# All stores of the last two turned blocks on SyncE's queue, and four operand rings of the w_up stage laid out in another order

## The chip, the cores and the metric

The kernel runs on one core of a Trainium2 chip. The metric is the device time of one launch in microseconds (us). Before the change it is 2649.21 us, the median of 3 runs that lie between 2648.27 and 2650.63 us.

## What is computed

One layer of an encoder on 2048 tokens of 1024 features, in float32. Cut to what this case needs:

```python
h  = rms_norm(x, norm_mix)
z  = h @ w_in                                  # queries, keys, values and gates of two attentions
yA = windowed_gqa(...)                         # window of 128 tokens
yB = neighborhood_attn(...)                    # on a 32 x 64 grid of tokens
merged = sigmoid(gA) * (yA @ w_proj_a) + sigmoid(gB) * (yB @ w_proj_b)
x  = x + merged @ w_out
h2 = rms_norm(x, norm_mlp)
x  = x + square(relu(h2 @ w_up)) @ w_down      # w_up is 1024 x 4096, w_down 4096 x 1024
out = rms_norm(x, norm_final)
```

## The kernel before

**Stages.** TensorE does the input projection and the attentions (to 1060 us of the span), the gated projections and w_out (matmuls named `pgl` until 1394.8 us), w_up (from 1395.0 to 2030 us) and w_down (2032 to 2642 us). The case is about the seam between w_out and w_up.

**Operands.** Every float32 factor is split in a high part (a rounding, ScalarE, `CAST` in the helper at L283) and a low part (what the rounding lost, VectorE, L284), and each 128x128 by 128x512 product is three matmuls: high by high (L287), high by low (L288), low by high (L289).

**w_up by seven products.** Tokens and features are taken as 2 by 2 blocks, and seven products of sums of blocks replace eight. For each half `m` of the tokens (1024 each) and each eighth `q` of w_up's 4096 columns, `up_quad` does the products in the order 1, 5, 6, 2, 7, 4, 3. A product is 24 matmuls: two PSUM banks, four slices, three matmuls. Its weights come from `up_left_steps` (tiles `uwhla`, `uwhlb`). Its other factor is a *page*, a pair of tiles `ubh` (high and low, each cast in two pieces), made by `up_right` once for each half `m`. In the listings below pages have these numbers: page 6 is 13477 and 13478, page 2 is 13485 and 13486, page 7 is 13563 and 13564, page 4 is 13571 and 13572, page 3 is 13577 and 13578. The weights of the first eighth's products 7, 4 and 3 are 13500, 13503 and 13507; `uwhlb_13825` is the weight of product 1 of the second eighth, made from the load `uraw_13583`. Banks 13643 and 13658 hold products 6, 7 and 4, and are read out between them (`uc`, L280).

**The turned blocks.** At the end of w_out the rows of x (`xr`, 128 tokens by 1024 features) are complete. Each is stored (`x2d`, L173, on ScalarE's queue), its squares are summed (L223, ScalarE, with a small VectorE and a GpSimd step), and it is scaled in place (L235, ScalarE). `turned_out` then transposes four rows on VectorE (L247) into a buffer of 4 KB a partition and stores that buffer as four pieces of 128 KB into `h2d` (L256), in runs of 512 bytes. For the third block of tokens (`turned_last(0, ...)`) the buffers are `m2` and `m3`, which w_out no longer needs; for the fourth (`turned_last(1, ...)`) they are `hu`. Each of these blocks has 16 such stores. `turned_last` gives two of each four to SyncE and two to ScalarE. What is stored is read again only by the work for the second half of the tokens.

**Who lies over what.** The rings of w_up are taken from the space that w_out's buffers leave. When `m0` to `m3` and `pgl` are closed, pages 6 and 2, `rb` and `c` take that space, so page 6 can be written once the stores of the third block have landed. When `hu` and `xr` are closed, `up_homes` makes four rings there, one below the other: pages 7, 4 and 3 and the small buffers `chunk`. A tile of a new ring waits for whatever still uses the old bytes.

**Order.** Each engine works through its instructions in the order in which a scheduler put them when the program was built, and an instruction that waits holds up all behind it on its engine. A DMA that SyncE or ScalarE issues takes the next of eight semaphores (`DMAHW0` to `DMAHW7`) in turn and waits until the DMA that had it before has landed.

Of the kernel before, what the change touches and what calls it, by code (L numbers as in the profile page):

```python
# [92 lines left out]
def encoder_layer(ctx, tc, x, norm_mix, w_in, b_gate, sink, rpb, w_pa, w_pb, w_out,  # L93
                  norm_mlp, w_up, w_down, norm_final, dist_a, mask_b, out):
    nc = tc.nc
    V, A, G, PE, SY = nc.vector, nc.scalar, nc.gpsimd, nc.tensor, nc.sync
# [27 lines left out]
    def T(pl, shape, dt, tag, bufs):  # L124
        n_t[0] += 1
        pl = pl[tag] if isinstance(pl, dict) else pl
        return pl.tile(shape, dt, tag=tag, bufs=bufs, name=f"{tag}_{n_t[0]}")
# [83 lines left out]
    last_dma = [None]  # L211
# [24 lines left out]
            else:  # L236
                V.tensor_scalar(t, t, rstd_of(pl, t, jp), float(D) ** 0.5, ALU.mult, ALU.mult)

    def turned_out(d, ht, tiles, g, gain=None, queue=None):

        hv = ht.rearrange("p (j t c) -> p t j c", j=8, t=4)
        for t in range(4):
            V.transpose(out=hv[:, t], in_=tiles[t][:, g * 256 : (g + 1) * 256].rearrange("p (j c) -> p j c", j=8))  # L247
        h3 = ht.rearrange("p (j x) -> p j x", j=8)
        if gain is not None:
            (step, n), _ = gain.ap  # L250
            gv = bass.AP(gain.tensor, gain.offset + 8 * g, [[step, n], [1, 8], [0, P]])
            V.tensor_tensor(out=h3, in0=h3, in1=gv, op=ALU.mult)
        dv = d.rearrange("(j i) (a x) -> a i j x", i=32, a=4)
        for a in range(4):
            q = queue[a % 2] if queue else SY
            last = q.dma_start(dv[a][:, 8 * g : 8 * g + 8], h3[32 * a : 32 * a + 32]).ins  # L256
            if q is SY:
                last_dma[0] = last

    def turned_gain(t, norm):  # L260

        for a in range(4):
            SY.dma_start(t[32 * a : 32 * a + 32, 32:64], norm[0].rearrange("(j i) -> j i", i=32))
        V.transpose(out=t[:, 0:32], in_=t[:, 32:64])
        return t[:, 0:32]
# [29 lines left out]
    def ring(stack, tag, shape, dt, bufs, side="right"):  # L295

        pl = pool(f"r_{tag}", side=side, stack=stack)
        return lambda: T(pl, shape, dt, tag, bufs)
# [45 lines left out]
    def x_tiles(pl, b, bufs):  # L344
        out = []
        for t in range(4):
            xt = T(pl, [P, D], F32, "xin", bufs) if t < bufs else in_v2[0]()
            if b > 1:

                for a in range(4):  # L350
                    r = b * BT + a * P + t * 32
                    SY.dma_start(xt[32 * a : 32 * a + 32], xf[r : r + 32])
            else:
                r = b * BT + t * P
                last_dma[0] = SY.dma_start(xt, xf[r : r + P]).ins
            out.append(xt)
        return out
# [201 lines left out]
    tiles = [x_tiles(xp, 0, 8), None]  # L559
# [143 lines left out]
    for q in range(2, len(QUADS)):  # L703
        prep = iter(())
        if q in (2, 3):
            prep = wo_parts(q - 2, own_v)
        elif q in (7, 8):
            prep = wo_parts(q - 5, own_x)
        next(prep, None)
        if q == 5:  # L710
            s_v.close()
            in_v2.pop()
            xp = {**pools(s_z, "right", ("xin",), "x2"), "st": cp}
        if q == 7:
            bias_tables()
        lf = list(in_left(ws, 256, (1, 2) if q == 2 else (), ORDER if q == 2 else ORDER_3))
        if q + 1 < len(QUADS):
            ws = in_weights(*QUADS[q + 1])
        if q in (5, 6):

            b = q - 3
            xt = x_tiles(xp, b, 3)
            normalised(xp, xt, Junk(), by_scalar=True)
        ops2.extend(lf if q == 2 else ())
        for n, _ in enumerate(quad2 if q == 2 else in_seeded(*QUADS[q], iter(lf), right)):
            for _ in range(2 if q == 8 else 1):
                next(prep, None)
            if q in (5, 6) and n < 4:
                turned_out(h1d[b - 2], in_e().rearrange("p k x -> p (k x)"), xt, n)
        for _ in prep:  # L730
            pass
# [381 lines left out]
    h2d = [dp.tile([D, BT], F32, name=f"h2d{b}") for b in range(NB)]  # L1113
# [7 lines left out]
    gain = turned_gain(T(p4x, [P, P], F32, "gt", 1), norm_mlp)  # L1121
# [17 lines left out]
    def up_homes(*tags):  # L1139
        made = {}  # L1140
        for t in tags:
            shape, dt, bufs = {"raw": (PAGE, F32, 5), "whla": ([P, 2, 4, 256], F32R, 1), "whlb": ([P, 2, 4, 256], F32R, 2),
                               "S": ([P, 4, 256], F32, 2), "rb": (PAGE, F32, 1), "chunk": ([P, BT], F32, 4),
                               "c": ([P, BT], F32, 11)}.get(t, (PAGE, F32R, 2))
            made[t] = ring(s_up, f"u{t}", shape, dt, bufs)
            if t[:2] == "bh":
                up_page[int(t[2])] = made[t]
        up_rings.update(made)
# [303 lines left out]
    def beside_out(m):  # L1452

        loads = load_y(1) if m == 0 else up_start()
        for n in range(7):
            if m == 0 and n in (1, 3, 4, 6):
                state["y"] = next(loads)
            elif m == 1:
                if n < 2:
                    rows[1].extend(x_row(m, 1, 2 * n + t) for t in range(2))  # L1460
                elif n < 5:
                    next(loads)
                elif n == 6:
                    free = [T(p4x, [P, 2, 2, BT], F32, f"m{t}", 1).rearrange("p a b c -> p a (b c)") for t in (2, 3)]
                    turned_last(0, lambda g: free[g // 2][:, g % 2])
            yield
# [5 lines left out]
    def turned_last(i, own):  # L1472

        for g in range(4):
            turned_out(h2d[2 + i], own(g), rows[i], g, queue=(SY, A))

    state = {"y": next_y}
    rows = None
    for m in range(2):
# [5 lines left out]
        old, rows = rows, [[], []]  # L1485
# [23 lines left out]
        for f in range(8):  # L1509
            if m:  # L1510
                i = f // 4
                turned_out(h2d[i], T(p4x, [P, 2 * BT], F32, "ht", 1), old[i], f % 4, gain)
            if 0 < f and f + early < 8:
                gated(f + early, 0)
            gated(f, 1)
            add(V, ms[f // 2][:, f % 2], gates[f, 0], gates[f, 1])
            if f == 3:
                ready = [next(operands), next(operands)]
            if f >= 4 or m == 0:
                rows[1 - f // 4 if m else f // 4].append(x_row(m, 1 - f // 4 if m else f // 4, f % 4))  # L1520
# [19 lines left out]
    for _ in rest:  # L1540
        pass
    turned_last(1, lambda t: hu())
    s_hu.close()
    s_wo.close()
    up_homes("bh7", "bh4", "bh3", "chunk")
    for m in range(2):
        if m:
            right = next(rights)
# [30 lines left out]
    rows = [ring(s_dn, tag, [P, BT], F32, 8) for tag in "XYZW"]  # L1579
# [107 lines left out]
    for n in (1, 6, 2, 7, 5, 3, 4):  # L1687
        for group in ((range(8),) if n != 4 else (range(4), range(4, 8))):
# [8 lines left out]
            last = []  # L1697
# [54 lines left out]
```

## Time and profile before

| | |
|---|---|
| median of 3 runs | 2649.21 us (2648.27 to 2650.63) |
| the profiled execution | 2652.0 us, of which the span of its instructions is 2650.2 us |
| mean granted clock of TensorE | 0.993 |
| TensorE matmul, busy | 2578.1 us, 97% of the span |
| VectorE, busy | 1625.9 us, 61% |
| ScalarE, busy | 1293.3 us, 49% |
| the longest wait of TensorE in the program | 15.3 us, once, at 1416.9 us of the span |

Times are microseconds from the start of the span. In a row of the timeline the first number is the start, the second the length; `x8` is the number of instructions merged in the row, and the brackets tell how long the engine sat idle before it and what ended that. `SPq` and `ACTq` rows are DMAs being issued by SyncE and ScalarE. TensorE's records overlap (a matmul of 0.39 us is followed by the next after 0.23 us).

### The profile page before, as it was taken

What the parts mean: (1) busy time and instruction counts of PE and PEld (TensorE: products, weight loads), DVE (VectorE), ACT (ScalarE), POOL (GpSimd) and SP (SyncE); (2) the same over time, 40 slices, a digit from 0 to 9 for tenths busy, and PEclk for the clock granted to TensorE, in tenths of its full rate; (3) what the DMA queues carried; (4) which work ended last, traced back from release to release, by engine and by line L of the source; (5) the groups of instructions that cost most, each with busy time, mean ns of one, the idle gap of its engine ahead of it and who ended that gap; (6) DMA issues with size and microseconds to landing.
All of it is one profiled execution on the core that took longest, in us unless ns stands there. A gap on an engine that the chain in (4) does not pass through costs nothing.

```text
span 2650.2 us, 34483 instructions
## 1 busy us (share of the span) xinstructions
PE 2578.1 (97%) x12044; PEld 2138.1 (81%) x12044; DVE 1625.9 (61%) x2611; ACT 1293.3 (49%) x2319; POOL 376.5 (14%) x477
## 2 busy tenths in 40 slices
PE   7999999999999999999997999999999999999998
PEld 6878877787888887878885888888887888888887
DVE  7865566665444444566686676676666635555766
ACT  7345456666555555344245555554444332322444
POOL 0001233335555541000000000000000000000011
PEclk9999999999999999999998999999999999999999
DMA  5777784455876655777676655754437935445554
GB/s 183 247 245 200 235 284 142 113 141 159 226 221 190 189 163 152 249 253 256 198 273 218 222 203 199 278 200 156 145 119 264 322 110 179 143 148 174 183 190 168
DMA packets 349950, 525.94 MB, mean 198 GB/s; under 512 B 29624, under 2 KB 173112, under 8 KB 347600
## 3 DMA queue, kind: packets, MB, share of 16 engines
q1 hardware_dynamic: 328656, 481.79, 56.6%
q10 hardware_dynamic: 17600, 30.42, 3.2%
q0 software_dynamic: 3520, 11.54, 1.2%
q8 instruction: 95, 1.56, 0.2%
q14 instruction: 79, 0.65, 0.1%
HBM read 349.51 MB, written 174.13 MB: 198 GB/s over the span
## 4 chain that ended last, share of the span: by engine, by line
PE 79%; DMA 7%; DVE 5%; ACT 2%; issue 2%; SPq 1%; POOL 0%; ACTq 0%; POOLq 0%; DVEq 0%
PE b L288 15%; PE b L289 15%; PE b L287 15%; PE mm L201 4%; PE mm L200 4%; PE mm L202 4%; PE b L200 2%; PE av L1033 2%; PE b L201 2%; PE b L202 2%; PE zb L289 2%; PE zb L287 2%; PE zb L288 2%; PE s L994 2%; PE pt L1022 2%
## 5 line engine op out<-in xcount | busy, mean ns | idle before, releaser
L288 PE MATMUL b<-dwh,dah 128*128 128x512 f32 x896 | 348.7, 389 | 0.4 <-DVE dwh L284 0.4
L289 PE MATMUL b<-dwh,dah 128*128 128x512 f32 x896 | 347.7, 389 | 0.0
L287 PE MATMUL b<-dwh,dah 128*128 128x512 f32 x896 | 338.3, 389 | 1.7 <-ACT dwh L283 1.7
L283 ACT CAST dah<-da 128x1024 fp32r<-128x1024 f32 (+1 forms) x128 | 121.1, 947 | 368.2 <-PE b L289 246.7
L284 DVE TENSOR_TENSOR dah<-da,dah 128x1024 fp32r<-128x1024 f32 (+1 forms) x128 | 139.4, 1091 | 219.6 <-ACT dah L283 212.8
L287 PE MATMUL b<-ubh,uwhlb 128*128 128x512 f32 x592 | 232.4, 393 | 20.3 <-ACT ubh L283 15.3
L288 PE MATMUL b<-ubh,uwhlb 128*128 128x512 f32 x592 | 232.2, 392 | 0.0
L289 PE MATMUL b<-ubh,uwhlb 128*128 128x512 f32 x592 | 230.8, 391 | 0.0
L200 PE MATMUL mm<-hT,whl 128*128 128x512 f32 x544 | 219.4, 404 | 3.2 <-ACT hT L757 3.2
L201 PE MATMUL mm<-hT,whl 128*128 128x512 f32 x544 | 215.4, 396 | 0.6 <-DVE hT L758 0.6
L202 PE MATMUL mm<-hT,whl 128*128 128x512 f32 x544 | 215.5, 396 | 0.0
L287 PEld LDWEIGHTS b<-dwh,dah 128*128 128x128 f32 x896 | 168.1, 188 | 36.9 <-ACT dwh L283 2.1
L288 PEld LDWEIGHTS b<-dwh,dah 128*128 128x128 f32 x896 | 168.2, 188 | 35.7 <-DVE dwh L284 0.8
L289 PEld LDWEIGHTS b<-dwh,dah 128*128 128x128 f32 x896 | 168.2, 188 | 34.9
L287 PE MATMUL zb<-zh,zwhl 128*128 128x512 f32 x476 | 186.7, 393 | 5.7 <-DVE zc L280 2.3
L289 PE MATMUL zb<-zh,zwhl 128*128 128x512 f32 x476 | 185.5, 391 | 1.3 <-DVE zwhl L284 1.3
L288 PE MATMUL zb<-zh,zwhl 128*128 128x512 f32 x476 | 186.7, 392 | 0.0
L280 DVE TENSOR_TENSOR uc<-b,uc 128x512 f32<-128x512 f32 x160 | 109.1, 689 | 121.5 <-PE b L289 113.4
L287 PEld LDWEIGHTS b<-ubh,uwhlb 128*128 128x128 f32 x592 | 112.2, 190 | 44.8 <-ACT ubh L283 15.7
L288 PEld LDWEIGHTS b<-ubh,uwhlb 128*128 128x128 f32 x592 | 112.1, 189 | 24.0 <-DVE ubh L284 0.8
L289 PEld LDWEIGHTS b<-ubh,uwhlb 128*128 128x128 f32 x592 | 112.2, 189 | 23.5
L200 PEld LDWEIGHTS mm<-hT,whl 128*128 128x128 f32 x544 | 103.0, 189 | 21.7 <-ACT hT L757 4.1
(268 smaller groups left out, 5840.4 us busy)
## 6 DMA issues: line engine op xcount, KB each, us to landing
at<-uc SPq DMA_DIRECT2D x224, 256.0 KB
da<-at SPq DMA_DIRECT2D x96, 512.0 KB
dw<-in_w_down_dram SPq DMA_DIRECT2D x160, 256.0 KB
uraw<-in_w_up_dram SPq DMA_DIRECT2D x32, 1024.0 KB
pgl<-wo_d SPq DMA_DIRECT2D x28, 1024.0 KB
raw<-in_w_in_dram SPq DMA_DIRECT2D x34, 512.0 KB
zraw<-in_w_in_dram SPq DMA_DIRECT2D x16, 1024.0 KB
z<-zg SPq DMA_DIRECT2D x64, 256.0 KB
```

The lines of the kernel that those rows point to most:

```text
L200: PE.matmul(ps, lh, rh, start=first, stop=False)
L201: PE.matmul(ps, lh, rl, start=False, stop=False)
L202: PE.matmul(ps, ll, rh, start=False, stop=last)
L280: return eng.tensor_tensor(out=out, in0=a, in1=b, op=op).ins
L283: A.copy(hi, src)
L284: return eng.tensor_tensor(out=lo, in0=src, in1=hi.bitcast(F32), op=ALU.subtract).ins
L287: PE.matmul(ps, lh, rh, start=first, stop=False, skip_group_check=True)
L288: PE.matmul(ps, lh, rl, start=False, stop=False, skip_group_check=True)
L289: PE.matmul(ps, ll, rh, start=False, stop=last, skip_group_check=True)
L994: PE.matmul(ps[:, :n], q[:, i, :], kv[:, z, B_R0[i] // 4 : (B_R0[i] + B_NR[i]) // 4, 4 * B_C0[j] : 4 * (B_C0[j] + w)], start=z == 0, stop= ...
L1022: PE.transpose(pt[:kp, at + (i - i0) * P : at + (i - i0 + 1) * P], s[i][:, rr : rr + kp], ident)
L1033: last = PE.matmul(po[:, i0 * P : (i0 + ni) * P], v[:kp, c, :], src[:kp, o : o + ni * P], start=first, stop=(c == 7 and z == 1), skip_grou ...
```

## The change

Two edits. `turned_out` no longer takes a queue: all its stores go to SyncE, so that the 16 of 32 stores of the last two blocks that ScalarE issued are now SyncE's, and the variable `last_dma`, which the first loads of w_up's second eighth are made to follow, now names the very last of them. And the four rings are made in another order: page 3 and the small buffers come first and take the place over `hu` that page 7 had, and pages 7 and 4 take what lies below it, over `xr` and the rest.

```diff
-    def turned_out(d, ht, tiles, g, gain=None, queue=None):
+    def turned_out(d, ht, tiles, g, gain=None):
...
         for a in range(4):
-            q = queue[a % 2] if queue else SY
-            last = q.dma_start(dv[a][:, 8 * g : 8 * g + 8], h3[32 * a : 32 * a + 32]).ins
-            if q is SY:
-                last_dma[0] = last
+            last_dma[0] = SY.dma_start(dv[a][:, 8 * g : 8 * g + 8], h3[32 * a : 32 * a + 32]).ins
...
         for g in range(4):
-            turned_out(h2d[2 + i], own(g), rows[i], g, queue=(SY, A))
+            turned_out(h2d[2 + i], own(g), rows[i], g)
...
-    up_homes("bh7", "bh4", "bh3", "chunk")
+    up_homes("bh3", "chunk", "bh7", "bh4")
```

The scheduler puts the instructions around the seam in another order. Lines of the changed kernel are three lower from `turned_out` on (L283 is L280 there). Three places matter.

**ScalarE, end of w_out, first place.** Before, behind the third block's last scaling (`xr_12843`), the rows of the fourth block are `xr_12862` to `xr_12940`:

```order
L235 ACTIVATE xr_12843<-xr_12843,st_13264 128x1024
L256 DMA h2d_10823<-m_1576_13333 32x8x128 x4
L256 DMA h2d_10823<-m_1577_13334 32x8x128 x4
L173 DMA x2d_111<-xr_12862 128x1024
L173 DMA x2d_111<-xr_12864 128x1024
L173 DMA x2d_111<-xr_12938 128x1024
L173 DMA x2d_111<-xr_12940 128x1024
L223 ACTIVATE junk_13424,st_13423<-xr_12862 128x512
L283 CAST ubh_1587_13477<-uraw_13096 128x1024 x2
```

With the change:

```order
L173 DMA x2d_111<-xr_12862 128x1024
L223 ACTIVATE junk_13424,st_13423<-xr_12862 128x512 x2
L173 DMA x2d_111<-xr_12864 128x1024
L223 ACTIVATE junk_13431,st_13430<-xr_12864 128x512 x2
L235 ACTIVATE xr_12862<-xr_12862,st_13423 128x1024
L173 DMA x2d_111<-xr_12938 128x1024
L223 ACTIVATE junk_13438,st_13437<-xr_12938 128x512
L235 ACTIVATE xr_12864<-xr_12864,st_13430 128x1024
L223 ACTIVATE junk_13438,st_13437<-xr_12938 128x512
L173 DMA x2d_111<-xr_12940 128x1024
L223 ACTIVATE junk_13445,st_13444<-xr_12940 128x512 x2
L1337 COPY uc_13600<-b_13587 128x512
```

The eight stores are gone from ScalarE, and the summing and scaling of the fourth block's rows stands ahead of page 6's cast (13477), which comes right behind these rows.

**ScalarE, first eighth of w_up, second place.** With the waits that each row carries. Before:

```order
L256 DMA h2d_10824<-hu_13537 32x8x128 [waits DMAHW7_49]
L283 CAST ubh_1606_13577<-uraw_13471 128x1024 x2
L1311 ACTIVATE uc_13701<-uc_13701 128x512 [waits Activation_49]
L283 CAST ubh_1602_13563<-uraw_13094 128x1024 [waits DMAHW4_49,DMAHW5_49,DMAHW3_49,DMAHW6_49,DMAHW2_49,DMAHW7_49,DMAHW1_49,DMAHW0_49]
L283 CAST ubh_1602_13563<-uraw_13094 128x1024
L283 CAST ubh_1604_13571<-urb_13483 128x1024 x2
L283 CAST uwhlb_13825<-uraw_13583 128x1024 [waits DMAHW0_49,PE_49]
```

With the change:

```order
L280 CAST ubh_1602_13563<-uraw_13094 128x1024 [waits DVE_49,Activation_49]
L280 CAST ubh_1602_13563<-uraw_13094 128x1024
L280 CAST uwhlb_13503<-uraw_13113 128x1024 [waits PE_49]
L280 CAST ubh_1604_13571<-urb_13483 128x1024 [waits DVE_49]
L280 CAST ubh_1606_13577<-uraw_13471 128x1024 [waits DMAHW4_49,DMAHW5_49,DMAHW3_49,DMAHW6_49,DMAHW2_49,DMAHW7_49,DMAHW1_49,DMAHW0_49]
L280 CAST ubh_1606_13577<-uraw_13471 128x1024
L1307 ACTIVATE uc_13685<-b_13587 128x512 [waits PE_49]
L280 CAST uwhla_13507<-uraw_13113 128x1024 [waits PE_49,Activation_49]
L1307 ACTIVATE uc_13701<-b_13602 128x512
L280 CAST ubh_1604_13571<-urb_13483 128x1024 [waits DVE_49]
L1308 ACTIVATE uc_13685<-uc_13685 128x512 [waits Activation_49]
L1308 ACTIVATE uc_13701<-uc_13701 128x512 [waits Activation_49]
```

The wait for all eight DMA semaphores, that is for the stores out of `hu`, has moved from page 7 (13563) to page 3 (13577), and page 7 stands ahead of it. The row that follows is the cast of `uwhlb_13825`.

**TensorE, between products 7 and 4 of the first eighth, third place.** Before, the end of product 7 and the beginning of product 4:

```order
L288 MATMUL b_13658<-ubh_1603_13564,uwhlb_13500 128x512
L289 MATMUL b_13658<-ubh_1602_13563,uwhlb_13500 128x512
L287 MATMUL b_13643<-ubh_1604_13571,uwhlb_13503 128x512
L288 MATMUL b_13643<-ubh_1605_13572,uwhlb_13503 128x512
L289 MATMUL b_13643<-ubh_1604_13571,uwhlb_13503 128x512
```

With the change:

```order
L285 MATMUL b_13658<-ubh_1603_13564,uwhlb_13500 128x512
L286 MATMUL b_13658<-ubh_1602_13563,uwhlb_13500 128x512
L284 MATMUL b_13859<-ubh_1551_13099,uwhlb_13825 128x512
L285 MATMUL b_13859<-ubh_1552_13100,uwhlb_13825 128x512
L284 MATMUL b_13874<-ubh_1551_13099,uwhlb_13825 128x512
L285 MATMUL b_13874<-ubh_1552_13100,uwhlb_13825 128x512
L284 MATMUL b_13643<-ubh_1604_13571,uwhlb_13503 128x512
```

Four matmuls of the second eighth's product 1 now stand ahead of product 4, and the rest of that product 1 stands ahead of and behind product 3.

## The prediction

> **What bounds the kernel now.** The page's first part says that TensorE is the bound nearly everywhere:
>
> ```profile
> PE 2578.1 (97%) x12044; PEld 2138.1 (81%) x12044; DVE 1625.9 (61%) x2611; ACT 1293.3 (49%) x2319; POOL 376.5 (14%) x477
> ```
>
> So an edit off TensorE can only win where TensorE waits. I read TensorE's table of waits next (total, times, longest). The first row is its longest wait, and both rows belong to the seam:
>
> ```profile
> PE b L287 <- ACT ubh L283: 15.3, 1, 15.3
> PE b L287 <- DVE uc L280: 3.3, 1, 3.3
> PE b L287 <- ACT dwh L283: 1.7, 1, 1.7
> ```
>
> TensorE's timeline there; each row kept begins or ends a product of the first eighth (6 from 1405.86, 2 from 1411.30, 7 from 1432.21, 4 from 1443.14, 3 from 1451.60):
>
> ```profile
> 1405.86 0.39 PE L287 MATMUL b<-ubh,uwhlb 128*128 128x512 f32 x1
> ...
> 1411.30 0.39 PE L287 MATMUL b<-ubh,uwhla 128*128 128x512 f32 x1
> ...
> 1416.51 0.39 PE L289 MATMUL b<-ubh,uwhla 128*128 128x512 f32 x1
> 1432.21 1.22 PE L287 MATMUL b<-ubh,uwhlb 128*128 128x512 f32 x2 [15.31 <-ACT ubh L283]
> ...
> 1443.14 0.76 PE L287 MATMUL b<-ubh,uwhlb 128*128 128x512 f32 x1 [3.35 <-DVE uc L280]
> ...
> 1451.60 0.39 PE L287 MATMUL b<-ubh,uwhla 128*128 128x512 f32 x1
> ```
>
> An unhindered product takes 1411.30 - 1405.86 = 5.44 us, a matmul 0.227. Product 2 is out at 1416.74 and product 3 begins at 1451.60: 34.86 us for products 7 and 4, which need 10.88. **24.0 us are lost here**, and that is the most the change can win at this place: 18.7 us of idling, and 5.3 us because the matmuls behind each gap run slowly. The windows of one microsecond show that (in each row: window, length, busy time of each engine, granted clock, DMA share, GB/s):
>
> ```profile
> 1442.00:1443.00 1.00, 0.00 (x0) 0.00 (x0) 1.00 (x3) 0.00 (x0) 0.00 (x0) 0.74 1.06 410
> 1444.00:1445.00 1.00, 1.00 (x4) 0.71 (x4) 1.00 (x3) 0.78 (x2) 0.00 (x0) 0.50 1.06 391
> ```
>
> Who held page 7? ScalarE's and SyncE's timelines:
>
> ```profile
> 1386.31 7.95 ACTq L256 DMA_DIRECT2D h2d<-m  x8
> 1394.35 5.72 ACTq L173 DMA_DIRECT2D x2d<-xr  x4
> ...
> 1400.74 1.99 ACT L283 CAST ubh<-uraw 128x1024 fp32r<-128x1024 f32 x2
> ...
> 1406.69 1.05 ACT L283 CAST ubh<-urb 128x1024 fp32r<-128x1024 f32 x1 [0.19 <-DMA urb<-h2d]
> 1407.64 1.15 ACT L235 ACTIVATE xr<-xr,st 128x1024 f32<-128x1024 f32 x1
> ...
> 1422.26 5.65 ACTq L256 DMA_DIRECT2D h2d<-hu  x5
> 1427.96 1.99 ACT L283 CAST ubh<-uraw 128x1024 fp32r<-128x1024 f32 x2 [6.03 <-DMA h2d<-hu]
> ...
> 1431.11 2.00 ACT L283 CAST ubh<-uraw 128x1024 fp32r<-128x1024 f32 x2 [0.63 <-DMA h2d<-hu]
> ```
>
> ```profile
> 1386.30 7.88 SPq L256 DMA_DIRECT2D h2d<-m  x8
> 1394.89 0.38 SPq L1247 DMA_DIRECT2D urb<-h2d  x1
> 1420.35 7.49 SPq L256 DMA_DIRECT2D h2d<-hu  x8
> 1427.93 1.92 SPq L1161 DMA_DIRECT2D uraw<-in_w_up_dram  x2
> ```
>
> ScalarE does nothing but issue stores from 1386.31 to 1400.07, so the fourth block is scaled late and its stores start only at 1420.35. Issuing ScalarE's half of them keeps it from casting until 1427.9 (the row of 5.65 us), and page 7's cast, the one at 1431.11, waits for the last landing. Three things in a row: late start, 10.8 us from first issue to last landing, and a page that is needed next.
>
> **The change part by part.**
>
> *The third block's 16 stores, all on SyncE.* ScalarE loses 7.95 us of issuing. Its four `x2d` stores can then go out as rows are complete (VectorE's last addition to the first row begins at 1388.38), beside SyncE's stores instead of behind them.
>
> ```profile
> 1388.38 0.69 DVE L280 TENSOR_TENSOR xr<-b,xr 128x512 f32<-128x512 f32 x1 [0.53 <-PE b L289]
> ...
> 1418.58 2.72 DVE L247 STREAM_TRANSPOSE hu<-xr 128x256 f32<-128x256 f32 x8
> ```
>
> ```profile
> 1386.30:1394.30 8.00, 8.00 (x37) 6.60 (x36) 3.62 (x7) 0.00 (x0) 0.00 (x0) 1.00 0.87 203
> 1400.10:1406.50 6.40, 6.40 (x30) 5.31 (x29) 3.51 (x4) 6.39 (x13) 0.55 (x1) 1.00 0.83 335
> 1261.30:1263.30 2.00, 2.00 (x11) 1.65 (x10) 1.11 (x3) 0.00 (x0) 0.00 (x0) 1.00 1.09 350
> ```
>
> The DMA engines are busy throughout (0.87, then 0.83), so the same bytes take the same time whatever queue they are on. The 16 stores, four `x2d` and the load of `urb` end at 1406.5 now (its cast waits 0.19 us to 1406.69); 1 MB at 335 GB/s is 3.1 us, so without `urb` the rest ends at about 1403.4. The third block's last store lands between 1397 (the `x2d` stores all behind it, as now) and 1403.5 (all beside it). I take **1403.5**, since three `x2d` stores are issued before its last one. Page 6's cast then moves from 1400.74 to 1403.5. Its first low half follows 0.95 + 1.14 us later, at 1405.7, and TensorE wants it at 1405.86: cost 0, up to 1 us. SyncE's load of `urb` (1394.89 now) goes out behind eight more stores, up to 5 us later, and lands no later than 1406.5, since the DMA engines have no less and no more to move; page 2's cast is not up before 1409.0 (below). If it landed after that, each microsecond would delay all that follows on ScalarE.
>
> *One queue against two* is what the trace doesn't show for 16 stores in a row. The bounds are the pieces' own rows (ns: shortest, median, longest):
>
> ```profile
> L256 SPq DMA_DIRECT2D h1d<-ze x32: 322/512/1547, 234.7 to 277.2; - x32
> L256 SPq DMA_DIRECT2D h2d<-ht x32: 302/462/1210, 1221.1 to 1289.2; - x32
> ...
> L256 SPq DMA_DIRECT2D h2d<-hu x8: 302/1006/1187, 1420.4 to 1426.9; - x8
> ```
>
> With two queues each takes 1.0 us a store, 0.5 us together; SyncE alone, with the same shape, takes 0.46 to 0.51. I take 0.6 a store and the landing as it is, 10.8 us; ends: 0.46 and 1.55 us a store. The Trainium skill ("DMA: Bandwidth & Descriptors", section "Issuing engines are not separate DMA queues") says that transfers issued by several engines share the same 16 DMA engines and that more issuers save only issue time; the window at 1261.3, SyncE's queue alone with share 1.09, agrees, and by that rule the landing term stays 10.8 us.
>
> *The fourth block.* On ScalarE, behind 1403.5: page 6 (two casts, 1.9), scaling (1.06, L235 from 1407.64 less its overlap), a weight cast (0.95), a copy (0.5), the last scaling (1.06): 1409.0. VectorE's transposes are 2.72/8 = 0.34 us each; with the work ahead of them the first store goes at about **1409.8** instead of 1420.35, and the last lands at 1409.8 + 10.8 = 1420.6; I take 1421.
>
> *Page 7 no longer waits for it.* Its casts stand behind page 2's two and a weight, so at 1409.0 + 1.9 + 0.95 = 1411.9 to 1413.8; TensorE is not free before 1416.74, and the 15.3 us go. What is late next? First product 2: VectorE now has the fourth block's transposes (to about 1410.7) and a subtraction ahead of page 2's low half, each 1.14 us, done at about 1413.0, and TensorE wants it at 1411.5: 1.4 us. Product 7's second bank loses some 0.3 us. Then product 4, which stands behind four matmuls on `uwhlb_13825`. Its cast is the last of ScalarE's row from page 3 on: page 3 at 1421 (1.9), two L1310 (0.5 each), a weight (0.95), the second half of page 4 (0.95), two L1311 (0.55 each), then itself (0.95): 1427.9, TensorE at 1428.2. TensorE is ready at 1416.74 + 1.7 + 5.44 = 1423.9. **4.3 us** of waiting. The load behind that cast is no later: SyncE issues it behind 16 stores, as it does now at 1427.93, so at about 1418, and 1 MB lands by 1425.
>
> *Clock.* A gap of 3.35 us now makes product 4 last 1451.60 - 1443.14 = 8.46 us, 3.0 too long; I charge the 4.3 us with 3.0. The Trainium skill ("TensorE: Matmul & The Clock Gate", "What's actually happening") gives windows of about 3.4 us, a whole idle one halving the clock and a busy one restoring it; by that the price would be 1.7 us, and the row of half a clock at 1444 shows the longer stretch.
>
> *The second wait*, 3.35 us for `uc` behind VectorE's additions for the load, loses its place: product 4 gets its banks while it waits for `uwhlb_13825`. *The small buffers* over `hu` are first loaded in the second eighth, behind all this: 0. In w_down a few loads and additions change places; the only wait there is the 1.7 us in the table, so between -1.7 and +1.7, taken as 0. Behind the seam TensorE has no wait until w_down that the table shows, so what is won stays won.
>
> *Sum.* Lost then: 1.4 + 0.3 + 4.3 + 3.0 = 9.0 us instead of 24.0; gain 15.0. The profiled execution takes 2652.0 us (its span 2650.2), 2.8 above the median; 2637.0 on its scale, **2634** on the median's 2649.2.
>
> **The rivals.** *Nothing is late next* (chance 0.11): scalings and casts run ahead of my chain and the waits are 1 to 2 us, too short for the clock; gain 21 to 24, time about 2627. For it: page 7's wait is gone. Against: the order puts the second eighth's weight ahead of product 4.
>
> *One queue takes its own pace, mildly* (0.12): 1.0 us a store, the median of a queue in the bursts; the fourth block lands 16 x 0.4 = 6.4 us later, all of it in product 4's wait; gain 9, time 2640 to 2644.
>
> *The wait only moves* (0.07): the change doesn't do what it says. At 1.2 us a store the third block lands 4 us later too, page 6 stalls product 6, and about 24 us are lost again: within 0.2%, which is about what a measurement of this kernel can tell from no change.
>
> *Slower* (0.05): the same mechanism past its turning point. Beyond 1.1 us each further 0.1 us a store costs 32 x 0.1 = 3.2 us, so it decides from 1.3; at 1.55, the longest `h1d` store, 8 us are lost on top: 2657. Against it: the medians of SyncE alone.
>
> **How the numbers follow.** Forecast 2634 with 0.65, its own range 2630 to 2639. The range 2627 to 2643 adds about half of the first rival and most of the second: 0.8. Faster by over 0.2% (below 2643.9): 0.65 + 0.11 + 0.12 = 0.88; within 0.07; slower 0.05.
>
> **What would show it.** After the change: no 15.3 us wait in TensorE's table; one of 3 to 6 us before the second eighth's first matmul, ended by ScalarE's cast, and about 1.4 us in product 2; the fourth block's stores issued from about 1410; page 6 cast at about 1403.5; a half clock for some 6 us about 1428. A first store out of `hu` behind 1415, or SyncE's 16 stores taking over 12 us, would make the prediction wrong; no wait at product 4 would make it too slow.

## The result, and the profile after

The changed kernel takes 2635.79 us (median of 5 runs, 2633.13 to 2637.51), beside 2649.21 us (5 runs, 2643.85 to 2652.87) for the kernel before on the same chip. The ratio is 0.9949, with a 95% interval of 0.9935 to 0.9964: 13.4 us faster, and between 9.5 and 17.2. The forecast was 2634. The profiled execution takes 2636.0 us (its span 2634.2, mean granted clock 0.996), 16.0 us less than the profiled execution of before.

TensorE's busy time is the same to 1.1 us, and its share of the span is higher. From the page's first part, and from TensorE's table of waits (total, times, longest):

```profile
PE 2577.0 (98%) x12044; PEld 2138.2 (81%) x12044; DVE 1626.5 (62%) x2611; ACT 1290.9 (49%) x2319; POOL 374.1 (14%) x477
...
PE b L284 <- ACT uwhlb L280: 4.4, 1, 4.4
...
PE b L285 <- DVE ubh L281: 1.7, 2, 1.2
PE b L284 <- ACT dwh L280: 1.7, 1, 1.7
```

The 15.3 us for page 7 and the 3.3 us for `uc` are gone. One wait of 4.4 us has come, for a weight, and two short ones in products 6 and 2. TensorE's timeline shows where they stand:

```profile
1405.31 0.50 PE L285 MATMUL b<-ubh,uwhlb 128*128 128x512 f32 x1 [0.57 <-DVE ubh L281]
...
1412.46 0.51 PE L285 MATMUL b<-ubh,uwhla 128*128 128x512 f32 x1 [1.17 <-DVE ubh L281]
...
1417.62 0.39 PE L284 MATMUL b<-ubh,uwhlb 128*128 128x512 f32 x1
...
1423.12 0.39 PE L286 MATMUL b<-ubh,uwhlb 128*128 128x512 f32 x1
1427.87 0.80 PE L284 MATMUL b<-ubh,uwhlb 128*128 128x512 f32 x1 [4.36 <-ACT uwhlb L280]
1428.46 0.63 PE L285 MATMUL b<-ubh,uwhlb 128*128 128x512 f32 x1
...
1432.73 0.40 PE L285 MATMUL b<-ubh,uwhlb 128*128 128x512 f32 x1
```

Product 7 begins at 1417.62 with no wait. TensorE is out of it after 1423.12 and stands until 1427.87 in front of the second eighth's first matmul. Then 11 matmuls take 4.86 us, to 1432.73, instead of 2.50 (0.227 each): the half clock, which a window of one microsecond shows as 0.50 (columns as in the prediction):

```profile
1431.00:1432.00 1.00, 1.00 (x4) 0.79 (x3) 1.00 (x2) 0.64 (x2) 0.00 (x0) 0.50 1.01 330
```

Who holds the weight? ScalarE's and SyncE's timelines:

```profile
1402.95 2.00 ACT L280 CAST ubh<-uraw 128x1024 fp32r<-128x1024 f32 x2 [2.61 <-DMA h2d<-m]
...
1407.31 1.15 ACT L235 ACTIVATE xr<-xr,st 128x1024 f32<-128x1024 f32 x1
1408.37 1.98 ACT L280 CAST ubh<-urb 128x1024 fp32r<-128x1024 f32 x2
...
1411.21 2.00 ACT L280 CAST ubh<-uraw 128x1024 fp32r<-128x1024 f32 x2
...
1417.58 1.05 ACT L280 CAST ubh<-urb 128x1024 fp32r<-128x1024 f32 x1 [3.43 <-DVE urb L277]
1420.97 2.01 ACT L280 CAST ubh<-uraw 128x1024 fp32r<-128x1024 f32 x2 [2.34 <-DMA h2d<-hu]
...
1424.78 1.04 ACT L280 CAST ubh<-urb 128x1024 fp32r<-128x1024 f32 x1
...
1426.77 1.04 ACT L280 CAST uwhlb<-uraw 128x1024 fp32r<-128x1024 f32 x1
```

```profile
1384.80 14.16 SPq L255 DMA_DIRECT2D h2d<-m  x16
1399.07 1.51 SPq L1244 DMA_DIRECT2D urb<-h2d  x1
1409.22 9.43 SPq L255 DMA_DIRECT2D h2d<-hu  x16
1418.75 1.56 SPq L1158 DMA_DIRECT2D uraw<-in_w_up_dram  x3
```

ScalarE scales the fourth block's last row at 1407.31, and the first store out of `hu` goes at 1409.22 (1420.35 before). Page 7 is cast at 1411.21, with nothing to wait for. Page 3 now has the wait that page 7 had: its cast stands until the stores have landed at 1420.97, and behind it in ScalarE's row come the rest of page 4 (1424.78) and the weight (1426.77).

**A measure for the experiments.** The w_up stage has the same 2688 matmuls in every kernel, and what lies behind the seam doesn't change: its last 2400 matmuls take 545.7 to 545.8 us in all twelve traces. So the time from the start of its first matmul to the start of its last one holds what a kernel loses at the seam, without what the run did before it. Its first and its last row, of before and then of after:

```profile
1394.98 0.39 PE L287 MATMUL b<-ubh,uwhla 128*128 128x512 f32 x1
...
2030.06 0.39 PE L289 MATMUL b<-ubh,uwhla 128*128 128x512 f32 x1
```

```profile
1393.47 0.39 PE L284 MATMUL b<-ubh,uwhla 128*128 128x512 f32 x1
...
2014.03 0.39 PE L286 MATMUL b<-ubh,uwhla 128*128 128x512 f32 x1
```

That is 635.1 us before and 620.6 after, 14.5 less. The other 1.5 us of the 16.0 between the two executions arose ahead of the seam (1394.98 against 1393.47), and ahead of the first store that the edits touch (1386.30 before, 1384.80 here). w_down gives nothing back and takes nothing: its wait for `dwh` is 1.7 us in both tables.

### The profile page after: what moved, and what is told of

Its sections match the earlier page's. It is cut to its first block, busy times and chain, and to the rows that moved or that the text cites. A ratio compares the mean times of both kernels' runs of the same rounds, so it can differ in the third digit from the quotient of the medians.

```text
span 2634.2 us, 34479 instructions
## 1 busy us (share of the span) xinstructions
PE 2577.0 (98%) x12044; PEld 2138.2 (81%) x12044; DVE 1626.5 (62%) x2611; ACT 1290.9 (49%) x2319; POOL 374.1 (14%) x477
## 5 line engine op out<-in xcount | busy, mean ns | idle before, releaser
L280 ACT CAST dah<-da 128x1024 fp32r<-128x1024 f32 (+1 forms) x128 | 120.8, 945 | 368.3 <-PE b L286 250.3
```

The lines of the kernel that those rows point to most:

```text
L280: A.copy(hi, src)
```

## The experiments

Theory, as the prediction had it: three holds stand in a row (the fourth block is scaled late, its stores take 11 us, and page 7, which is needed next, waits for them); both edits shorten the row, and what is left is ScalarE's row behind page 3. First rival: the order of the rings does it, since it takes the wait from page 7. Second rival: ScalarE's time does it, since it is free of 13.6 us of issuing, wherever the wait stands.

The two edits are three: the third block's stores (line T below), the fourth block's (F), and the rings (R). All combinations were run. `w_up` is the measure above, from the first start to the last in each kernel's own trace; the wait is TensorE's longest at the seam. Each ratio is against the kernel before on the same chip, where its medians are 2649.21 (the change), 2648.38 (F alone, T alone), 2649.19 (the change, run again) and 2648.36 (the others); the ratios are worked out from all runs and differ from the quotient of the medians by up to 0.0006.

| kernel | median us | ratio (95% interval) | w_up: first, last, length | longest wait at the seam |
|---|---|---|---|---|
| before | 2649.21 | 1 | 1394.98, 2030.06, 635.1 | 15.31, page 7 |
| R alone | 2645.75 | 0.9988 (0.9978 to 0.9998) | 1393.74, 2022.94, 629.2 | 10.47, page 7 |
| F alone | 2645.17 | 0.9990 (0.9982 to 0.9999) | 1395.88, 2025.41, 629.5 | 15.06, page 7 |
| T alone | 2637.57 | 0.9961 (0.9948 to 0.9973) | 1394.01, 2015.58, 621.6 | 3.49, page 7 |
| T and F | 2640.05 | 0.9964 (0.9950 to 0.9977) | 1393.34, 2015.64, 622.3 | 4.09, page 7 |
| T and R | 2636.09 | 0.9949 (0.9932 to 0.9966) | 1393.92, 2016.30, 622.4 | 1.74, page 7's low half |
| F and R | 2634.78 | 0.9946 (0.9929 to 0.9963) | 1396.50, 2015.36, 618.9 | 4.58, page 7 |
| the change (T, F and R) | 2635.79 | 0.9949 (0.9935 to 0.9964) | 1393.47, 2014.03, 620.6 | 4.36, the weight |
| the change, run again | 2636.95 | 0.9957 (0.9944 to 0.9971) | 1394.90, 2014.99, 620.1 | 4.09, the weight |

The profiled execution of before lies 2.8 us above its median, and the lengths of w_up show gains 1 to 4 us larger than the ratios do, in all but one kernel (T and R). Each length is from one execution; the changed kernel's two differ by 0.5 us.

### The rings alone

```diff
-    up_homes("bh7", "bh4", "bh3", "chunk")
+    up_homes("bh3", "chunk", "bh7", "bh4")
```

> The kernel before with the new order of the rings alone; the stores stay split over SyncE and ScalarE. Main theory (the time is set by when the fourth block's stores land and by which product needs the page that waits for them; both edits together only won because the stores came 10.5 us earlier): ScalarE still issues the third block's stores and then eight of the fourth block's, until about 1428, and page 7's casts stand behind that issuing, so TensorE waits about 12 us for page 7 instead of 15.3, and product 4 keeps a wait of 2 to 3 us; gain 1 to 6 us, 2643 to 2648 us. Rival 1 (the ring order does it: page 7 no longer waits for the stores, the queue adds little): no wait over 5 us, about 2636 us. Rival 2 (ScalarE's 13.6 us of issuing are what is won, wherever the wait stands): no gain, 2649 us.

0.9988: 3.2 us, between 0.5 and 5.8. The first rival falls. ScalarE's timeline (the two rows of stores that are left out, x2 and x1, begin at 1417.44):

```profile
1419.34 5.66 ACTq L256 DMA_DIRECT2D h2d<-hu  x5
1425.04 1.99 ACT L283 CAST ubh<-uraw 128x1024 fp32r<-128x1024 f32 x2 [6.03 <-DMA h2d<-hu]
1426.94 1.99 ACT L283 CAST ubh<-urb 128x1024 fp32r<-128x1024 f32 x2
1429.36 1.98 ACT L283 CAST ubh<-uraw 128x1024 fp32r<-128x1024 f32 x2
```

Page 7 no longer waits for the last landing, but its cast (1425.04) stands in ScalarE's row behind eight stores that ScalarE issues itself: it starts 0.04 us behind the last of them (1419.34 + 5.66), and that row is late. (The DMA in the bracket is what the profile infers; page 3's cast, at 1429.36, is the one that this order of the rings makes wait for the stores.) TensorE waits 10.47 us, and 2.91 us at product 4. So a buffer that is free helps little while the instruction that would use it queues behind the late work on its engine.

### The two queues alone, with the old rings

```diff
-    up_homes("bh3", "chunk", "bh7", "bh4")
+    up_homes("bh7", "bh4", "bh3", "chunk")
```

(in the changed kernel)

> The changed kernel with the old order of the rings: all stores on SyncE, page 7 over the fourth block's buffers as before. Main theory: the stores still go out from about 1409 and land at about 1421, so page 7's cast is done about 1422 and TensorE waits about 4 us in front of product 7, where it waited 15.3; the half clock behind it costs some 2 us more, and the weight of the second eighth is then no later than TensorE, so the 4.4 us wait of the changed kernel is gone. Lost in all 8 to 10 us, as with both edits: 2634 to 2639 us. Rival 1 (the ring order does it): a wait of over 10 us for page 7 stays, 2643 to 2649 us. Rival 2 (ScalarE free of issuing): 2636 us, as the main theory.

0.9964, and w_up 622.3. The wait for page 7 is there again, and it is 4.09 us long; the 4.36 us for the weight have shrunk to 1.14. TensorE's timeline:

```profile
1422.29 1.22 PE L284 MATMUL b<-ubh,uwhlb 128*128 128x512 f32 x2 [4.09 <-ACT ubh L280]
...
1431.73 0.50 PE L284 MATMUL b<-ubh,uwhlb 128*128 128x512 f32 x1 [1.14 <-ACT uwhlb L280]
```

The first wait is the expected one; the second was expected to be gone. The median, 2640.05, is 1 us above the range expected for it. The rings added to this are worth 1.7 to 2.2 us of w_up (622.3 against 620.6 and 620.1), which the ratios, with intervals that overlap, can't confirm: in the main they only move a wait of 4 us from page 7 to the weight.

### The fourth block on two queues, and the third block on two queues

The kernel before with the new rings, and in the first run the third block's stores alone on SyncE, in the second the fourth block's alone:

```diff
-            turned_out(h2d[2 + i], own(g), rows[i], g, queue=(SY, A))
+            turned_out(h2d[2 + i], own(g), rows[i], g, queue=(SY, A) if i else None)
```

```diff
-            turned_out(h2d[2 + i], own(g), rows[i], g, queue=(SY, A))
+            turned_out(h2d[2 + i], own(g), rows[i], g, queue=None if i else (SY, A))
```

> New order of the rings, the third block's stores all on SyncE, the fourth block's split over SyncE and ScalarE as before. Main theory: the fourth block is scaled as early as in the changed kernel, first store at about 1409, last landing at about 1420 to 1421 whether one queue carries them or two; ScalarE's issuing holds page 7's casts to 1417 to 1420, a wait of 0 to 3 us before product 7, then 3 to 5 us behind page 3; 2635 to 2639 us. Rival 1 (ring order): 2636 us. Rival 2 (issuing time on ScalarE): half the issuing is back, so half the gain, about 2643 us.

> New order of the rings, the third block's stores split over SyncE and ScalarE as before, the fourth block's all on SyncE. Main theory: the fourth block is scaled late again, first store at about 1420, last landing at about 1431; page 7's casts do not wait for that but stand behind the late scaling, done at about 1423 to 1424, so TensorE waits about 7 us before product 7 and pays about 3 us of half clock; page 3, at 1433, is needed about then: 2636 to 2641 us. Rival 1 (ring order): no wait over 5 us, 2636 us. Rival 2 (issuing time on ScalarE): half the gain, about 2643 us.

0.9949 and 0.9946. With either half of ScalarE's issuing back, the whole gain stays, where the second rival expected half of it; it falls in this form. The second of these runs is the surprise. ScalarE's timeline there:

```profile
1421.91 1.98 ACT L283 CAST ubh<-uraw 128x1024 fp32r<-128x1024 f32 x2
1423.80 2.00 ACT L283 CAST ubh<-urb 128x1024 fp32r<-128x1024 f32 x2
1430.88 2.01 ACT L283 CAST ubh<-uraw 128x1024 fp32r<-128x1024 f32 x2 [5.09 <-DMA h2d<-hu]
```

The fourth block is as late as before (first store at 1419.93), and its last store lands at 1430.88. But page 7 (1421.91) waits neither for the landing nor behind issuing, so TensorE waits 4.58 us (7 were expected), and page 3 at 1430.88 is in time for product 3. An early start is thus not needed, if page 7's cast waits neither for the stores to land nor behind their issuing; what is left of its wait is ScalarE's late scaling ahead of it.

### One block's queue alone, with the old rings

The same two edits of `turned_last`, with the rings of before: the fourth block alone, then the third alone.

> The kernel before with the fourth block's stores alone on SyncE; third block split, old order of the rings. Main theory: the fourth block is scaled late, its first store goes at 1418 to 1420 and the last lands 11 us later, and page 7 waits for that landing: TensorE waits 12 to 15 us before product 7, gain 0 to 4 us, 2645 to 2649 us. Rival 2, in the form that the last runs leave it (what counts is that ScalarE does not issue the fourth block's stores): the gain is there without the rings, 2636 us.

> The kernel before with the third block's stores alone on SyncE; fourth block split, old order of the rings. Main theory: the fourth block is scaled early, its first store goes at about 1410 and the last lands at about 1421; page 7 waits for that landing and is cast at once: TensorE waits about 4 us before product 7, as with both blocks on SyncE and the old rings; 2636 to 2641 us. Rival 2, in the form that the last runs leave it (ScalarE's issuing of the fourth block's stores holds page 7): no gain, 2645 to 2649 us.

0.9990 and 0.9961. TensorE's longest wait at the seam in the first, from the table of waits, and the two in the second, from the timeline:

```profile
PE b L287 <- ACT ubh L283: 15.1, 1, 15.1
```

```profile
1421.61 1.22 PE L287 MATMUL b<-ubh,uwhlb 128*128 128x512 f32 x2 [3.49 <-ACT ubh L283]
...
1431.68 0.50 PE L287 MATMUL b<-ubh,uwhlb 128*128 128x512 f32 x1 [1.14 <-ACT uwhlb L283]
```

With the fourth block's queue alone, page 7 still waits for stores that begin at 1420.87, so the second rival falls in its later form too. That w_up is 5.6 us shorter in its trace all the same (the ratio gives 2.6) comes from the second wait: the 3.35 us for `uc` and the slow matmuls behind them are gone, since VectorE reads product 4's bank at 1440.72, ahead of its second sum for the load, where before it read behind that sum, at 1442.31. With the third block's alone, the fourth block is scaled early, its first store goes at 1409.59 and page 7's cast starts at 1420.52, as soon as the last has landed. One of the three edits, the third block's queue, therefore wins by itself what the change wins, within the intervals; and the other two together win it without that one. They are two ways to the same gain, and their gains don't add up.

### What is left: the wait of 4.4 us

Three kernels take it apart, each built on the one ahead of it. First the second eighth's product 1 goes behind product 4 in TensorE's order (`fourth` holds the last matmul of the first eighth's product 4):

```diff
+                    with tc.issue_after(fourth[0]) if m == 0 and q == 1 and n == 1 else nullcontext():
-                    mm3s(ps, hl[:, 0, k, at], ...)
+                        mm = mm3s(ps, hl[:, 0, k, at], ...)
```

> The changed kernel, with the second eighth's product 1 put behind product 4 in TensorE's order; ScalarE's and VectorE's orders stay as they are. Main theory (what is left at the seam is the wait for the weight of those four matmuls, whose cast ends ScalarE's row behind page 3, and the half clock behind that wait): the 4.4 us wait goes; product 4 starts at once and meets the second half of page 4, whose high part is cast at 1425.7 and whose low part VectorE ends at 1427.8 in the changed kernel, so two shorter waits of about 1 and 2 us take its place, too short for much half clock. Lost about 4.8 us in place of 8.4: 2631 to 2633 us. Rival (the weight only happens to be named there; page 3 or ScalarE's whole row is as late for product 4): the same wait of over 4 us stands in product 4, 2636 us.

0.9961 (0.9947 to 0.9975), 2638.13 us, w_up from 1398.82 to 2020.07, 621.3: nothing is won, as the rival had it, though the wait is 3.35 us instead of over 4 and hangs on VectorE.

```profile
1432.72 0.76 PE L284 MATMUL b<-ubh,uwhlb 128*128 128x512 f32 x1 [3.35 <-ACT uc L1308]
```

That is product 4's own first matmul. The releaser that the row names is a small ScalarE instruction, but this matmul's wait in the built program is for ScalarE and VectorE, and VectorE's timeline fits it: the bank has to be read first (`uc`, to 1432.58), and the reading stands behind the low half of page 3 and a weight.

```profile
1428.48 2.35 DVE L281 TENSOR_TENSOR ubh<-uraw,ubh 128x1024 fp32r<-128x1024 f32 x2
1430.75 1.22 DVE L281 TENSOR_TENSOR uwhla<-uraw,uwhla 128x1024 fp32r<-128x1024 f32 x1
1431.89 0.69 DVE L277 TENSOR_TENSOR uc<-b,uc 128x512 f32<-128x512 f32 x1
```

This is the wait for the same reading as in the kernel before, 3.35 us there and here, but other work stands ahead of the reading: before, it was VectorE's sums for the second eighth's load. In the changed kernel it lay under the wait for the weight: the same reading ends at 1426.70 there (VectorE, 0.69 from 1426.01), 1.1 us ahead of the weight's cast (1426.77 + 1.04).

Then page 3's casts go behind page 4's on ScalarE, which also takes the low half of page 3 from in front of that reading on VectorE (`cast` holds the last high cast):

```diff
-        parts(3, b22)
+        with tc.issue_after(cast[0]):
+            parts(3, b22)
```

> As the run before it, and page 3's casts put behind page 4's in ScalarE's order, so that no cast that product 4 needs stands behind the wait for the fourth block's stores. Main theory: page 4's second half is cast at about 1421 to 1422, its low part is done at about 1425.5, and product 4 waits under 1 us; page 3's casts end at about 1424 and its low half at 1427.8, before product 3 reaches it. Lost about 2.7 us: 2629 to 2632 us, the best of all. Rival (page 3's delay by a microsecond passes on to the second eighth's weight): a wait of 2 to 4 us before the second eighth's first matmul, 2633 to 2636 us.

0.9951 (0.9938 to 0.9963), 2634.48 us, w_up from 1390.37 to 2010.23, 619.9. The median is inside the range of the rival, and neither theory had the right place: product 4 waits 1.08 us, and the long wait has moved to product 3, behind VectorE again.

```profile
1427.43 0.72 PE L286 MATMUL b<-ubh,uwhla 128*128 128x512 f32 x1 [3.55 <-DVE uc L277]
```

```profile
1421.80 2.36 DVE L283 TENSOR_TENSOR ubh<-uraw,ubh 128x1024 fp32r<-128x1024 f32 x2
1425.46 1.23 DVE L277 TENSOR_TENSOR uS<-uraw,uraw 128x1024 f32<-128x1024 f32 x1 [1.31 <-DMA uraw<-in_w_up_dram]
1426.60 1.28 DVE L277 TENSOR_TENSOR uc<-b,uc 128x512 f32<-128x512 f32 x2
```

Product 3 adds to banks that VectorE must have read (`uc`, 1426.60). That reading stands behind `uS`, a sum for the second eighth, which waits for a load that SyncE issued behind the fourth block's stores. Third, `uS` and the second eighth's first weight go behind the reading (`read_out` holds product 7's last read-out):

```diff
-            lf = up_left(ws, page_done[0] if m == 0 and q == 1 else None) if q else lf
+            lf = up_left(ws, read_out[0] if m == 0 and q == 1 else None) if q else lf
```

> As the run with page 4 ahead of page 3, and VectorE's sum for the second eighth (uS) put behind its read-out of the banks that product 3 and product 4 go on with. Main theory, as the last two runs left it (at the seam the engines' rows are so full that each wait taken away uncovers the next; what came next there was a 3.6 us wait of product 3 for a read-out that stood behind uS, and uS behind a load): the 3.6 us wait and its half clock go; what stays is 1.15 us in product 2, about 1.1 at the first bank of product 4 and about 1 at product 3. w_up lasts about 615 us from its first to its last matmul, in place of 619.9 there and 620.6 in the changed kernel; 2629 to 2632 us. Rival (another wait of 3 us or more comes next, at the second eighth's first product): 619 to 621 us for w_up, 2634 to 2637 us.

> The changed kernel again, on the same chip as the run beside it, to compare the two there. Main theory: 2634 to 2638 us, the wait for the second eighth's weight between 4 and 5 us, w_up about 620 to 621 us. If the first profile's numbers at the seam were chance (rival), that wait is shorter or longer by over a microsecond.

0.9941 (0.9928 to 0.9953), 2631.9 us (2630.82 to 2633.52), w_up from 1393.19 to 2009.80, 616.6. The changed kernel beside it on the same chip: 2636.95 us (2635.12 to 2638.73). So this version beats both kernels, and the changed one by 5.1 us. What is left at the seam, from its table of waits:

```profile
PE b L286 <- DVE uc L277: 2.1, 2, 1.1
PE b L287 <- DVE ubh L283: 2.0, 2, 1.2
```

Four waits of at most 1.2 us, two of which were there in the changed kernel, and none of them followed by a half clock. The length of w_up, 616.6, is 1.6 us above what was expected for it. The wait for the weight in the changed kernel, run again, is 4.09 us, 0.3 off its first profile.

## Why the prediction was right

By its steps, on the changed kernel's trace:

- **The bound.** The seam was the place: w_up takes 14.5 us less, where 15.0 were forecast. The measured 13.4 us (9.5 to 17.2) hold both.
- **The third block's stores.** The prediction took 0.6 us a store, and for this block that was wrong: SyncE's row gives 14.16 / 16 = 0.89, and 0.85 to 1.03 in the eight runs that have it, beside four `x2d` stores (the DMA engines' share is 0.89 from 1384.8 to 1399.0). By the letter its sign "SyncE's 16 stores taking over 12 us" came true here. It did no harm, because the landing had not been worked out from that price but taken at the end of a range that the bytes gave: page 6 is cast at 1402.95, forecast 1403.5 (w_up begins 1.5 us earlier in this execution, so it is 1404.5 on the scale of before, 1.0 late). It costs product 6 an idle time of 0.57 us, 0.76 when run again, inside "0, up to 1".
- **The fourth block.** Here SyncE's row gives 9.43 / 16 = 0.59 us a store, and the three rivals that rest on 1.0 us and more for this block are out by that number. First store at 1409.22 (1410.7 on the scale of before), forecast 1409.8. First issue to landing: 1420.97 - 1409.22 = 11.75 us, forecast 10.8. One queue carries them in 10.9 to 11.8 us in the six runs that show it, two queues in 10.8 (before) and 10.9 (T alone). The Trainium skill ("DMA: Bandwidth & Descriptors", section "Issuing engines are not separate DMA queues") has a second issuer save issue time alone; for the fourth block these runs agree to within 1 us.
- **Product 2 and product 7.** 1.17 us of idle, forecast 1.4; at product 7's second bank 0.13, forecast 0.3.
- **The weight in front of product 4.** 4.36 us, and 4.09 when run again; forecast 4.3, from ScalarE's row behind the landing, which is as the prediction listed it. As a size the term was right, with some luck: on the scale of before, the weight's cast and TensorE's end of product 7 both came 1 to 1.5 us later than forecast. As a cause it was too narrow: with the four matmuls out of the way, 3.35 us for `uc` were there again, and after those 3.55 at product 3. The prediction let the wait for `uc` go because product 4 gets its banks while TensorE waits for the weight; that held, by about a microsecond. ScalarE's and VectorE's rows behind the landing are late as a whole, and the weight is only where TensorE met them.
- **Clock.** 2.36 us (4.86 - 11 x 0.227), and 1.7 when run again; 3.0 was charged. Of the terms in the sum this one was sized worst. The rival in which nothing is late next took waits of 1 to 2 us as "too short for the clock"; the last section shows that this doesn't always hold.
- **The rest.** w_down as forecast. By the starts of matmuls, w_up's first five products, product 4 and 18 matmuls of the next eighth take 1439.79 - 1393.47 = 46.3 us and need 162 x 0.227 = 36.8: 9.5 us are lost, 9.0 were forecast.

```profile
1439.79 0.39 PE L284 MATMUL b<-ubh,uwhla 128*128 128x512 f32 x1
```

What the prediction did not see is how its three holds combine. It let "the 15.3 us go" because page 7 no longer waits for the landing, and needed the early start only for page 3. Shown is that the early start alone takes page 7's wait from 15.31 to 3.49 with the old rings, and that the rings alone leave 10.47. The sum came out because the change leaves what either way alone leaves: one wait of some 4 us (3.49 with T alone, 4.58 with F and R, 4.36 with all three) and the clock behind it. These waits stand behind different things, the landing or the late scaling, and that they are about equal no run explains.

What stays open: why F and R without T has the shortest w_up of the eight (618.9). It is 1.2 to 1.7 us below the change, and the ratios don't separate them.

## What to carry to other kernels

When several holds stand in a row ahead of one wait, price each alone as well as all together: different edits may take the same gain, and the next one then only moves the wait. A buffer that becomes free earlier helps only if the instruction that fills it doesn't queue behind the late work on its engine; so read that engine's row up to the instruction, not its semaphore. And where a wait is ended by the last of a long row, removing that one reader uncovers the next: here it took three edits of order to turn 4.4 us and a half clock into two more waits of about 1 us.

## What the runs showed of the hardware

The price of the half clock behind a gap doesn't follow the gap's length. Worked out as above (matmuls until the pace is 0.227 again), it is 3.0 us behind 15.06 us of idle (F alone), 1.9 behind 15.31 and 3.0 behind 3.35 (both before), 3.1 behind 4.58 (F and R), 2.7 behind 4.09 (T and F), 1.7 behind 4.09 (the change, run again) and 1.7 behind 3.55 (page 4 first). Single gaps of 1.2 us and less cost 0.1, and so does one of 1.62 us that every kernel has later in w_up (1725.81 in the changed one). But short gaps close together can cost as much as a long one; from the kernel with T and R:

```profile
1421.12 0.50 PE L288 MATMUL b<-ubh,uwhlb 128*128 128x512 f32 x1 [1.74 <-DVE ubh L284]
...
1429.16 0.50 PE L287 MATMUL b<-ubh,uwhlb 128*128 128x512 f32 x1 [1.14 <-ACT uwhlb L283]
...
1431.72 0.64 PE L287 MATMUL b<-ubh,uwhlb 128*128 128x512 f32 x1 [1.37 <-DVE uc L280]
...
1433.44 0.63 PE L288 MATMUL b<-ubh,uwhlb 128*128 128x512 f32 x1
```

1.14 and 1.37 us, with four matmuls between them, are followed by matmuls at 0.43 us each, which cost 1.7 us in all; and so is a gap of 1.74 us ten microseconds ahead of them, with one of 0.25 us shortly before it. How close is close enough stays open: in the last version above, gaps of 1.08 and 1.03 us with twelve matmuls between them are not followed by a half clock. The Trainium skill ("TensorE: Matmul & The Clock Gate", section "What's actually happening") says that the windows of about 3.4 us run freely, and that full speed returns after a busy one. By that, as an estimate, half the speed for one to two such windows would cost 1.7 to 3.4 us, whatever the gap; the runs give 1.7 to 3.1, and the 1.7 that the prediction worked out from that page is the lower end. That the clock falls after an idle window of that length, as that section has it, is not what these two gaps show: from the start of the first to the end of the second, 3.7 us, TensorE was idle for 2.5.
